# Wider steps in a planned first stage: conditioning rows by three row blocks, a channel-major projection by two

## The chip, the cores and the metric

One core of one Trainium2 chip runs the kernel. The metric is device time in microseconds (us) for one execution. The engines are named as in the profile: PE is TensorE's matmul side and PEld its weight loads, DVE is VectorE, ACT is ScalarE, POOL is GpSimd, SP is SyncE, which here only issues DMA transfers.

## The reference

One decoder layer on 512 tokens of width 1024, float32. Cut to what the change touches:

```
mod = silu(c) @ w_ada + b_ada                 # 1 x 6144: shift1, scale1, gate1, shift2, scale2, gate2
h = rmsnorm(x) * (1 + scale1) + shift1
proj = h @ w_in                               # 1024 x 2824: DeltaNet q, k, v (1536), its gate z (512), attention q, k, v, ...
q, k, v = silu(causal_conv(proj[:, :1536]))   # then a chunked gated delta rule over 8 chunks of 64 tokens
o_sw = sliding_window_attention(...)          # the other head group
x = x + gate1 * (concat(o_dn * silu(z), o_sw) @ w_out)
h = rmsnorm(x) * (1 + scale2) + shift2
x = x + gate2 * moe(h)                        # top 4 of 32 experts, 12.6 MB of weights each
```

## The kernel before

**Two stages.** The first stage (everything up to line 1608) computes the mixer and the routing; the second (from line 1900) runs the 32 experts, whose weights it streams from HBM. Between them the first stage's memory pools are closed, and the second stage's gathers need the routing result.

**The planner.** From line 445 on the order of the first stage's work is not written out by hand. Each piece of work is a Python generator (a task). It yields either a list of keys that it must wait for, or a claim: an engine letter (P for PE, V for DVE, S for ACT, G for POOL, D for a DMA), a cost in us, and tags of buffers that it takes. Class `Flow` (lines 113 to 180) plays the tasks against a model of the engines when the program is built and emits instructions in the order in which the model starts them. Among the claims that could start within `SLACK` (0.1 us) of the earliest one, the lowest priority number wins (line 173). After a claim the task's next claim is ready only a latency later (0.12 us for PE, 2.5 us for a DMA, line 117), so that two tasks that are both ready on PE take turns, claim by claim. A claim is never broken up: what the generator emits between two yields stands together in the engine's queue. On the chip every engine then runs its own queue in that order and waits by semaphores for real data.

**The late conditioning rows.** `late_loads` (line 630) loads w_ada for rows 2 to 5 of the six (gate1, shift2, scale2, gate2), eight blocks of 128 x 1024 (512 KB) for each row, into six slots (tag `lp`); SP issues them (line 637). `late(r)` (line 640) multiplies them: for each block k four matmuls on column strips of 32 (the program has eight matmul instructions for them, as each float32 matmul is two), line 649, then four more (again eight instructions) for the bias at line 654, an evacuation on DVE and a small store. Each block is a claim of its own on PE (0.5 us in the model) and so is the bias (0.45 us). The four rows follow one another; row r + 1 starts after the store of row r. Priority 1. The attention's `swa_weights` (line 732) wait for `("late", 5)`, since their buffer is one of the late rows' slots.

**The channel-major projection.** `project(c0, j)` (line 559) makes 128 channels by 512 tokens: for each of eight row blocks k three matmuls (`mm3`, line 314, emitted at line 317: high x high, high x low, low x high parts in fp32r) of 128 x 128 by 128 x 512 into `ps_ch`. Each k is a claim of 0.66 us on PE. There are 16 such projections: twelve for q, k and v (`conv`, priority 5) and four for the gate z (`gate`, priority 2), so 128 claims and 384 matmuls. `win` (line 538) loads their weights in 1 MB pieces on SP (line 542) and splits them on ACT, DVE and POOL.

**Around them** in the same planned list: `inverse` (line 976; the 64 x 64 triangular inverses of the delta rule, five levels of three 32-instruction matmul groups at line 818, then line 1033 and line 1049), the attention (`swa_*`, priority 1), the recurrence over eight chunks (`recur`), the output projection (lines 1142 and 1161) and the routing (`route`, `ranks`, `places`).

Of the kernel before, what the change touches and what calls it, by code (L numbers as in the profile page):

```python
# [20 lines left out]
P = 128  # L21
# [3 lines left out]
KT = D // P  # L25
# [9 lines left out]
THEN, THEN1 = 2, 6  # L35
RINGS = {"w": RING2 - 1, "x": 1, "r": RING, "v": RING3 - 1, "vy": 1, "e": RINGE}
SLACK = 0.1
CONV_END = "V"
PR = {"swa": 1, "conv": 5, "cend": 4, "in": 4, "late": 1, "z": 2, "load": 1, "yS": 7, "fin": 3, "rt": 4, "yT": 3, "rec": 1, "oout": 2}
UBANKS = 6  # L40
# [72 lines left out]
class Flow:  # L113
# [40 lines left out]
    def run(self):  # L154
        while True:
# [15 lines left out]
            else:  # L171
                first = min(at for at, _ in can)
                at, t = min((c for c in can if c[0] <= first + SLACK), key=lambda c: (c[1][0], c[0], c[1][1]))
                eng, cost = t[3][0][0], t[3][1]
# [9 lines left out]
def layer_kernel(ctx: ExitStack, tc: tile.TileContext, A, out, probe=None):  # L184
    nc = tc.nc
    V, S, G, TE = nc.vector, nc.scalar, nc.gpsimd, nc.tensor
# [5 lines left out]
    def bc(ap, shape):  # L192
        return ap.to_broadcast(shape)
# [23 lines left out]
    def bank(tag, name):  # L217
        return {"a": ppA, "d": ppD, "s": ppS, "o": ppO}[tag].tile([P, 512], F32, name=name, tag=tag)
# [7 lines left out]
    def wk(tag, name, bufs, n=T):  # L226
        return pool_of(tag).tile([P, n], F32, name=name, tag=tag, bufs=bufs)
# [68 lines left out]
    def behind(late, early):  # L296

        tc.add_manual_dep(late.ins, early.ins.name,
                          mybir.DependencyInfo(mybir.DependencyClass.NoSync, mybir.DependencyReason.DATA), reason="order")
# [14 lines left out]
    def mm3(acc, w, x_, start, stop):  # L314

        for q, (a, b) in enumerate(((0, 0), (0, 1), (1, 0))):
            TE.matmul(acc, lhsT=w[a], rhs=x_[b], start=start and q == 0, stop=stop and q == 2)  # L317

    cact = ce.tile([P, 8], F32, name="cact")
# [34 lines left out]
    hx = []  # L354
# [62 lines left out]
    with tc.manual_schedule(engines={nc.vector.engine, nc.scalar.engine, nc.tensor.engine}):  # L417
        for k in range(KT + 1):
# [22 lines left out]
            if k:  # L441
                for i in range(NT):
                    tok_mm(i, k - 1)
                mm3(tg[0:8], [w[:, 0:8] for w in wtok[k - 1]], hx[k - 1], k == 1, k == KT)
    flow = Flow({"a": 2, "d": 3, "s": 2, "o": 1, "cv": 4, "sv": 2, "x": 4, "r": 3, "m": 7, "L0": 1, "L1": 1, "lp": 6, "room": 2, "kv": 2, "sm": 2,
                 "qS": 2, "on": 2})

    def tv(n):
        return 0.09 + 0.001 * n
# [73 lines left out]
    kTv, wins = {}, {}  # L523

    def sigmoid(a, e):

        yield "S", ts(T)
        S.activation(e, a, AF.Abs)
        yield "S", ts(T)
        S.activation(e, e, AF.Exp, scale=-1.0)  # L530
        yield "S", ts(T)
        S.activation(e, e, AF.Ln, bias=one1)
        yield "V", tv(T)
        V.scalar_tensor_tensor(e, a, 0.0, e, op0=OP.min, op1=OP.subtract)
        yield "S", ts(T)
        S.activation(e, e, AF.Exp)
# [22 lines left out]
    def project(c0, j):  # L559

        a = None
        for k in range(KT):
            yield [("win", c0, k // 4)]
            yield ("P", 0.66) + (("a",) if k == 0 else ())
            if a is None:
                a = bank("a", "ps_ch")
            mm3(a, [w[:, P * j:P * j + P] for w in wins[c0, k // 4][k]], hx[k], k == 0, k == KT - 1)
        return a

    def conv_end(a, ct, dst, key):  # L570
# [12 lines left out]
        yield from sigmoid(y, e)  # L583
        yield CONV_END, (tg_ if CONV_END == "G" else tv)(T)
        (G if CONV_END == "G" else V).tensor_tensor(dst, y.rearrange("p (n c) -> p n c", c=64), e.rearrange("p (n c) -> p n c", c=64), op=OP.mult)
        flow.give("cv", "cv")
        flow.mark(*key)

    def conv(p, name, c0, prio):

        ct = c0 // P
        dst = None
        for j in range(2):
            a = yield from project(c0, j)
            if j == 0:
                if name == "q":
                    dst = qT[:, p]
                else:
                    yield "N", 0.0, "kv"
                    dst = kTv[name, p] = wk("kv", name + "T", 2, D).rearrange("p (n e c) -> p n e c", n=8, e=2)  # L600
            flow.add(prio, conv_end(a, ct + j, dst[:, :, j, :], ("head", name, p, j)))
        flow.give("x", "x", "r")
# [10 lines left out]
    def gate(p, prio):  # L613

        yield [("values", 2, 1)]
        if p == 0:
            state["zT"] = big("z", "zT", 2).rearrange("p (h t) -> p h t", t=T)
        for j in range(2):
            a = yield from project(1536 + 256 * p, j)
            flow.add(prio, gate_end(a, 2 * p + j))  # L620
        flow.give("x", "x", "r")
        flow.mark("zmm", p)
# [5 lines left out]
    lw = {}  # L628
# [11 lines left out]
    def late(r):  # L640

        pa = None
        for k in range(KT):
            yield [("lw", r, k)]
            yield ("P", 0.5) + (("o",) if k == 0 else ())
            if pa is None:
                pa = bank("o", "ps_ada")
            for j in range(4):
                TE.matmul(pa[32 * j:32 * j + 32, :256], lhsT=bc(cact[:, k:k + 1], [P, 32]), rhs=lw[r, k][:, 256 * j:256 * j + 256],
                          start=(k == 0), stop=False)  # L650
            flow.give("lp")
        yield "P", 0.45
        for j in range(4):
            TE.matmul(pa[32 * j:32 * j + 32, :256], lhsT=bc(ident[0:24, 4 * r + j:4 * r + j + 1], [24, 32]), rhs=bada, start=False, stop=True)
        yield ("V", tv(256)) + (() if r == 5 else ("sv",))
        m = g2s if r == 5 else wk("sv", "mod", 2)[:, 0:256]
        if r == 4:
            V.scalar_tensor_tensor(m, pa[:, :256], 1.0, n2q, op0=OP.add, op1=OP.mult)
        else:
            V.tensor_copy(m, pa[:, :256])  # L660
        flow.give("o")
        yield "D", 0.5
        nc.sync.dma_start(modd[r - 2].rearrange("(j n) -> j n", n=256), m.rearrange("(j r) n -> j r n", r=32)[:, 0])
        if r != 5:
            flow.give("sv")
        flow.mark("late", r)
# [889 lines left out]
    lp = once.enter_context(tc.tile_pool(name="lp", reuse_waits="tile", bufs=1))  # L1556
# [3 lines left out]
    with tc.manual_schedule(engines={nc.vector.engine, nc.scalar.engine, nc.tensor.engine, nc.gpsimd.engine, nc.sync.engine}):  # L1560
# [31 lines left out]
        flow.add(PR["swa"], swa())  # L1592
        flow.add(1, late_loads())
        flow.add(PR["late"], chain(*(late(r) for r in range(2, 6))))
        flow.add(PR["z"], chain(*(gate(p, PR["z"]) for p in range(2))))
        flow.add(PR["load"], loads())
# [304 lines left out]
    with tc.manual_schedule(engines={nc.sync.engine, nc.tensor.engine, nc.vector.engine, nc.scalar.engine}):  # L1901
# [10 lines left out]
        for q in range(NE + 1):  # L1912
            if q < NE:
                r = ORDER[q]
# [29 lines left out]
            if q:  # L1944
                r = ORDER[q - 1]
# [55 lines left out]
```

## Time and profile before

| | us |
|---|---|
| runs shown | 1479.09, 1485.01, 1486.35; median 1485.01 |
| profiled execution, its own time | 1480.72 |
| its span in the trace | 1478.9 |
| PE busy | 1381.5 (93% of the span) |
| PEld busy | 601.3 (41%) |
| DVE busy | 563.8 (38%) |
| mean HBM traffic over the span | 325 GB/s |

The profiled execution's own time is 1.8 us more than its span. An engine's busy time counts instructions under way; matmuls overlap, so that the time a matmul takes from PE is best read from the distance between the starts of neighbours. In a wait row, the name before the arrow is who waited and the name behind it is what ended the wait.

### The profile page before, as it was taken

How to read it: one execution, taken by the hardware profiler on the slowest of the kernel's cores; microseconds unless marked ns; L12 is line 12 of the kernel's file. 1: busy time of each engine (PE TensorE's matmuls, PEld its weight loads, DVE VectorE, ACT ScalarE, POOL GpSimd, SP SyncE). 2: the span in 40 equal slices, each digit the busy share in tenths (PEclk: the TensorE clock that was granted, in tenths of full speed). 3: DMA queues.
4: the chain of work that ended last, by engine and by line, in shares of the span. 5: the costliest groups of instructions: out<-in, count | busy, mean ns of one | idle time of the engine just before them, and what ended most of it. 6: DMA issues, size and time to landing. Idle time of an engine off the chain costs nothing. (4 is left out here: it accounts for less than half of the span.)

```text
span 1478.9 us, 22303 instructions
## 1 busy us (share of the span) xinstructions
PE 1381.5 (93%) x8586; PEld 601.3 (41%) x8586; DVE 563.8 (38%) x1247; ACT 237.8 (16%) x542; POOL 261.1 (18%) x216
## 2 busy tenths in 40 slices
PE   4999999999879999979999999999999999999974
PEld 3766666765443333322333333333333333343311
DVE  6965567566853222212221231223321323232310
ACT  4354354442211000000000000000000000010000
POOL 2213133202331111101011101102110112211110
PEclk9999999999969999999999999999999999999976
DMA  9655300256349999999999999999998999999995
GB/s 302 212 200 204 113 29 30 58 214 277 116 152 407 409 387 402 396 391 412 411 412 400 379 419 394 384 409 393 410 367 349 403 348 404 393 418 415 414 415 229
DMA packets 104980, 476.16 MB, mean 322 GB/s; under 512 B 13992, under 2 KB 39556, under 8 KB 55714
## 3 DMA queue, kind: packets, MB, share of 16 engines
q1 hardware_dynamic: 91842, 453.16, 77.4%
q0 software_dynamic: 11952, 18.75, 5.5%
q10 hardware_dynamic: 1072, 2.70, 0.5%
q8 instruction: 75, 1.23, 0.3%
q14 instruction: 39, 0.32, 0.1%
HBM read 464.14 MB, written 17.22 MB: 325 GB/s over the span
## 5 line engine op out<-in xcount | busy, mean ns | idle before, releaser
L1760 PE MATMUL ps_up<-we,xTe 128*64 128x512 f32 (+1 forms) x3040 | 622.2, 607 | 21.2 <-DMA we<-in_w_up_dram 16.8
L1760 PEld LDWEIGHTS ps_up<-we,xTe 128*64 128x64 f32 (+1 forms) x3040 | 188.5, 132 | 394.2 <-issue 336.8
L1797 PE MATMUL ps_dn<-we,aT 128*64 128x512 f32 (+1 forms) x1848 | 316.0, 534 | 19.7 <-DMA we<-in_w_down_dram 10.9
L1797 PEld LDWEIGHTS ps_dn<-we,aT 128*64 128x64 f32 (+1 forms) x1848 | 103.7, 129 | 232.2 <-issue 187.2
L1805 POOL DMA_INDIRECT out_dram<-yv,si x52 | 81.7, 1571 | 649.7 <-DVE yv L1804 464.9
L1712 DVE COPY xTe<-ps_xTe 128x256 f32<-128x256 f32 (+3 forms) x35 | 17.5, 501 | 307.4 <-PE ps_xTe L1711 307.4
L1785 ACT COPY aT<-ps_aT 128x512 f32<-128x512 f32 (+1 forms) x52 | 26.0, 530 | 512.5 <-PE ps_aT L1783 509.1
L1769 DVE TENSOR_TENSOR hu<-ps_up,bb 128x512 f32<-128x512 f32 (+1 forms) x52 | 32.1, 617 | 198.8 <-PE ps_up L1760 198.8
L1804 DVE SCALAR_TENSOR_TENSOR yv<-ps_dn,sg,g2p 128x512 f32<-128x512 f32 x38 | 28.5, 751 | 188.3 <-PE ps_dn L1797 187.4
L1771 ACT ACTIVATE hu<-hu 128x512 f32<-128x512 f32 (+1 forms) x52 | 29.8, 573 | 269.4 <-DVE hu L1770 269.4
L1697 POOL MEMSET xg<- 64x1024 f32 (+3 forms) x35 | 37.2, 1084 | 186.0 <-PE ps_xTe L1711 185.8
L317 PE MATMUL ps_ch<-hhi,wih 128*128 128x512 f32 x128 | 58.5, 457 | 0.0
L317 PE MATMUL ps_ch<-hl,wih 128*128 128x512 f32 x128 | 50.8, 397 | 0.0
L317 PE MATMUL ps_ch<-hhi,wl 128*128 128x512 f32 x128 | 50.5, 395 | 0.0
L1720 DVE STREAM_SHUFFLE bb<-bias 128x1024 f32<-128x1024 f32 (+1 forms) x44 | 48.8, 1137 | 0.1
L1712 ACT COPY xTe<-ps_xTe 128x256 f32<-128x256 f32 (+3 forms) x35 | 15.1, 433 | 163.4 <-PE ps_xTe L1711 163.4
L1698 POOL DMA_INDIRECT xg<-h2d,gi x35 | 35.7, 1021 | 16.1 <-POOL xg L1697 8.1
L1711 PEld LDWEIGHTS ps_xTe<-cst,xg 64*128 64x128 f32 (+3 forms) x280 | 24.1, 142 | 32.3 <-issue 23.1
L1783 PEld LDWEIGHTS ps_aT<-cst,act 128*128 128x128 f32 x180 | 24.3, 208 | 28.6 <-issue 25.7
L1711 PE MATMUL ps_xTe<-cst,xg 64*128 64x64 f32 (+3 forms) x280 | 30.1, 249 | 5.1 <-DMA xg<-h2d,gi 2.2
L317 PEld LDWEIGHTS ps_ch<-hhi,wih 128*128 128x128 f32 x128 | 24.2, 189 | 23.2 <-issue 18.0
L1142 PE MATMUL ps_y<-wos,oS 128*128 128x512 f32 x64 | 33.3, 613 | 0.0
(392 smaller groups left out, 1389.0 us busy)
## 6 DMA issues: line engine op xcount, KB each, us to landing
we<-in_w_up_dram SPq DMA_DIRECT2D x256, 1024.0 KB
we<-in_w_down_dram SPq DMA_DIRECT2D x128, 1024.0 KB
wa<-in_w_ada_dram SPq DMA_DIRECT2D x16, 512.0 KB
wi<-in_w_in_dram SPq DMA_DIRECT2D x8, 1024.0 KB
wl<-in_w_ada_dram SPq DMA_DIRECT2D x12, 512.0 KB
oS<-in_w_ada_dram SPq DMA_DIRECT2D x10, 512.0 KB
LL<-in_w_ada_dram SPq DMA_DIRECT2D x10, 512.0 KB
wt<-in_w_in_dram SPq DMA_DIRECT2D x4, 776.0 KB
```

The costliest lines, as they stand in the source:

```text
L317: TE.matmul(acc, lhsT=w[a], rhs=x_[b], start=start and q == 0, stop=stop and q == 2)
L1142: TE.matmul(a, lhsT=oS[:, j, P * i:P * i + P], rhs=wo[j][:, 512 * hf:512 * hf + 512], start=(j == 0), stop=(j == 3))
L1697: G.memset(xg[:rows_], 0.0)
L1698: state["gather"] = G.indirect_dma_start(out=xg[:rows_], out_offset=None, in_=h2d, in_offset=bass.IndirectOffsetOnAxis(ap=gidx(g)[:rows_], ...
L1711: TE.transpose(pt[:, k, :rows_], xg[:rows_, 512 * hf + P * k:512 * hf + P * k + P], ident[:rows_, :rows_])
L1712: state["turned", hf] = (S.copy if hf else V.tensor_copy)(xt_[:, 4 * hf:4 * hf + 4, :rows_], pt[:, :, :rows_])
L1720: V.stream_shuffle(bbs[w].rearrange("p h n -> p (h n)"), b[w], [0] * 32)
L1760: TE.matmul(t[w * j:w * j + w], lhsT=lhsT, rhs=rhs, start=(k == 0), stop=(k == KT - 1))
L1769: V.tensor_tensor(g, pg, bbs[w][:, 0], op=OP.add)
L1771: S.activation(sgm, g, AF.Sigmoid, scale=1.702)
L1797: TE.matmul(py[u][w * j:w * j + w, 0:m], lhsT=aT[u][:, kt % nf, w * (kt // nf):w * (kt // nf) + w], rhs=wd[kt][:, m * j:m * j + m], start= ...
L1805: G.indirect_dma_start(out=outv[u[1]], out_offset=bass.IndirectOffsetOnAxis(ap=sidx, axis=0), in_=yv, in_offset=None, compute_op=OP.add, b ...
```

## The change

`late` claims PE three times for a row, not nine: for blocks 0 to 2, blocks 3 to 5, and blocks 6 and 7 together with the bias. It waits for all blocks of a step before the step, and gives their slots back in the step. Its prices in the model are 0.25 + 0.17 for each block. `project` claims PE four times, not eight, for two row blocks each at 1.45. Nothing else is edited; the matmuls, their operands and their order within a row or a projection stay.

```diff
+LATES = {0: 3, 3: 6, 6: 8}
...
     def project(c0, j):
         a = None
-        for k in range(KT):
+        for k in range(0, KT, 2):
             yield [("win", c0, k // 4)]
-            yield ("P", 0.66) + (("a",) if k == 0 else ())
+            yield ("P", 1.45) + (("a",) if k == 0 else ())
             if a is None:
                 a = bank("a", "ps_ch")
-            mm3(a, [w[:, P * j:P * j + P] for w in wins[c0, k // 4][k]], hx[k], k == 0, k == KT - 1)
+            for k_ in (k, k + 1):
+                mm3(a, [w[:, P * j:P * j + P] for w in wins[c0, k // 4][k_]], hx[k_], k_ == 0, k_ == KT - 1)
         return a
...
         pa = None
         for k in range(KT):
-            yield [("lw", r, k)]
-            yield ("P", 0.5) + (("o",) if k == 0 else ())
+            if k not in LATES:
+                continue
+            ks = range(k, LATES[k])
+            yield [("lw", r, k_) for k_ in ks]
+            yield ("P", 0.25 + 0.17 * len(ks)) + (("o",) if k == 0 else ())
             if pa is None:
                 pa = bank("o", "ps_ada")
-            for j in range(4):
-                TE.matmul(pa[32 * j:32 * j + 32, :256], lhsT=bc(cact[:, k:k + 1], [P, 32]), rhs=lw[r, k][:, 256 * j:256 * j + 256],
-                          start=(k == 0), stop=False)
-            flow.give("lp")
-        yield "P", 0.45
+            for k_ in ks:
+                for j in range(4):
+                    TE.matmul(pa[32 * j:32 * j + 32, :256], lhsT=bc(cact[:, k_:k_ + 1], [P, 32]), rhs=lw[r, k_][:, 256 * j:256 * j + 256],
+                              start=(k_ == 0), stop=False)
+                flow.give("lp")
         for j in range(4):
             TE.matmul(pa[32 * j:32 * j + 32, :256], lhsT=bc(ident[0:24, 4 * r + j:4 * r + j + 1], [24, 32]), rhs=bada, start=False, stop=True)
```

## Rows read from the trace of the kernel before

**Rows 1.** The page, busy time of each engine, with share of the span and instructions.

```profile
PE 1381.5 (93%) x8586; PEld 601.3 (41%) x8586; DVE 563.8 (38%) x1247; ACT 237.8 (16%) x542; POOL 261.1 (18%) x216
```

**Rows 2.** Busy time by stretch, each engine, then PE clock, DMA share, GB/s.

```profile
79.10:170.20 91.10, 90.13 (x1044) 57.98 (x1043) 54.87 (x104) 36.93 (x67) 22.71 (x14) 1.00 0.59 209
170.20:240.00 69.80, 67.17 (x534) 46.66 (x531) 51.05 (x109) 37.49 (x95) 24.79 (x20) 0.98 0.10 31
240.00:312.00 72.00, 71.43 (x730) 50.13 (x728) 37.95 (x79) 32.35 (x72) 11.51 (x9) 1.00 0.26 73
312.00:410.00 98.00, 92.09 (x505) 48.29 (x506) 71.99 (x214) 22.20 (x84) 22.30 (x17) 1.00 0.55 208
436.00:1479.00 1043.00, 986.84 (x5379) 341.50 (x5379) 269.14 (x543) 72.20 (x140) 148.98 (x123) 0.97 0.99 391
```

**Rows 3.** Waits of PE from 79 to 440 us, the longest: total, times, longest.

```profile
PE ps_rt L1196 <- DVE room L1192: 7.5, 4, 2.7
```

**Rows 4.** Start of the second stage: POOL and SP in order of time.

```profile
430.23 0.18 POOL L1904 COPY second<-eri 1x1 int32<-1x1 int32 x1
...
431.47 11.94 SPq L1654 DMA_DIRECT2D we<-in_w_up_dram  x6
```

**Rows 5.** Tile of late rows: ns min/median/max of one, first and last start.

```profile
L649 PE MATMUL ps_ada<-wl,cact x96: 378/391/404, 86.4 to 168.4; 128*32 128x256 f32 x96
...
L649 PE MATMUL ps_ada<-oS,cact x80: 378/391/403, 90.2 to 161.9; 128*32 128x256 f32 x80
...
L649 PE MATMUL ps_ada<-LL,cact x80: 378/390/404, 93.9 to 164.5; 128*32 128x256 f32 x80
...
L654 PE MATMUL ps_ada<-bada,cst x32: 374/386/398, 103.6 to 169.9; 24*32 24x256 f32 x32
```

**Rows 6.** PE in order of time (start, us, line): late, projection, late.

```profile
140.05 0.64 PE L649 MATMUL ps_ada<-LL,cact 128*32 128x256 f32 x8
140.62 0.50 PE L317 MATMUL ps_ch<-hhi,wih 128*128 128x512 f32 x1
...
141.51 0.64 PE L649 MATMUL ps_ada<-wl,cact 128*32 128x256 f32 x8
```

**Rows 7.** PE in order of time: column strips by one column.

```profile
403.00 0.24 PE L1506 MATMUL ps_cnt<-one,sums 128*32 128x1 f32 x8
403.18 1.13 PE L1161 MATMUL ps_y<-wod,oT 128*128 128x512 f32 x2
```

**Rows 8.** The page, groups: experts' matmuls on half the columns; busy, mean ns.

```profile
L1760 PE MATMUL ps_up<-we,xTe 128*64 128x512 f32 (+1 forms) x3040 | 622.2, 607 | 21.2 <-DMA we<-in_w_up_dram 16.8
```

**Rows 9.** The page, groups: a third of the channel-major projection's matmuls.

```profile
L317 PE MATMUL ps_ch<-hhi,wih 128*128 128x512 f32 x128 | 58.5, 457 | 0.0
```

**Rows 10.** PE in order of time: inside an uninterrupted projection, one row block apart.

```profile
110.62 0.40 PE L317 MATMUL ps_ch<-hl,wih 128*128 128x512 f32 x1
...
111.32 0.40 PE L317 MATMUL ps_ch<-hl,wih 128*128 128x512 f32 x1
```

**Rows 11.** PE in order of time: a projection's row block ahead of transposes.

```profile
284.18 0.50 PE L317 MATMUL ps_ch<-hhi,wih 128*128 128x512 f32 x1
...
284.98 0.60 PE L934 MATMUL ps_tm<-cst,kT 128*128 128x128 f32 x4
```

**Rows 12.** SP in order of time: two loads of a late row.

```profile
139.10 1.97 SPq L637 DMA_DIRECT2D LL<-in_w_ada_dram  x2
```

**Rows 13.** The stretch after the first one's issue, columns as in rows 2.

```profile
139.10:142.00 2.90, 2.90 (x51) 1.68 (x50) 1.89 (x3) 0.06 (x1) 0.77 (x1) 1.00 0.58 172
```

**Rows 14.** SP's waits, 50 to 320 us: total, times, longest.

```profile
SPq L542 <- DVE wl L307: 46.4, 4, 26.3
```

**Rows 15.** PE in order of time: first attention weights; inverse's last products.

```profile
175.00 0.72 PE L743 MATMUL ps_l<-kS,qS 64*128 64x128 f32 x8
...
291.96 1.09 PE L1033 MATMUL ps_u<-vv,XT 64*64 64x128 f32 x16
...
294.57 1.09 PE L1033 MATMUL ps_u<-vv,XT 64*64 64x128 f32 x16
```

## The prediction, made before the changed kernel was run

> **What bounds the kernel now.** I read the page first: PE is busy in 93% of the span, no other engine above 38% [rows 1]. An average over two unlike stages decides nothing, so the busy time by stretch comes next [rows 2]. The second stage, from about 436 us, keeps the DMA at 0.99 of its time and PE at 987 of 1043 us; the change does not touch it. In the first stage, where the change lies, PE is busy 90.1 of 91.1 us, 67.2 of 69.8, 71.4 of 72.0 and 92.1 of 98.0, while the DMA stands at 0.10 to 0.59. The waits say the same: the longest group in which PE waited between 79 and 440 us is 7.5 us, all of it in routing, long after the edited tasks [rows 3]. So up to 410 us the first stage takes as long as PE's queue takes, and PE time that goes should bring its end forward.
>
> Does the end of the first stage carry the end of the kernel? The second expert's weights are requested by SP at 431.47, right after POOL's copy at 430.23 of an index that routing makes [rows 4]. The stream that fills the second stage thus starts when the first ends, and what the first stage gains or loses should arrive whole at the end.
>
> **The change part by part.** No matmul is added or removed. What goes is PE's turning from one kind of work to another.
>
> *Late rows.* The instructions are 96 + 80 + 80 for the blocks and 32 for the bias, 288 in all [rows 5]. In order of time each group on PE has eight and none sixteen, so there are 36 visits, from 86.4 to 169.9 us. A visit takes 0.57 us from its start to the next task's (140.05 to 140.62) [rows 6]: 36 x 0.57 = 20.5 us. After the change there are 12 visits of three groups each (3 blocks, 3 blocks, 2 blocks and the bias). The trace shows no visit of three, so I split the 0.57 into entering and streaming. A visit of eight instructions of the same tile shape with one column each takes 0.18 us (403.00 to 403.18) [rows 7]: nearly all entering, hence streaming of about 0.39. The experts' matmuls give a second price: 622.2 us for 3040 is 0.205 us for 512 columns on half the array's columns [rows 8]; a late instruction has half the columns and a quarter of the array, so 0.051, and eight take 0.41. I take 0.42 a group and 0.15 for entering: 3 x 0.42 + 0.15 = 1.41, twelve times 16.9. **Gain 3.6 us.** The bounds: nothing, if three groups take 3 x 0.57 (a longer time is excluded, since 0.57 already holds all that a visit needs), and 20.5 - 12 x 0.76 = 11.4, if the code's new price of 0.76 were true. I stay near rows 7 and 8, which agree.
>
> *Projection.* 128 row blocks, three matmuls each [rows 9]. Uninterrupted, one block follows the last after 0.70 us (110.62 to 111.32) [rows 10]. Alone between two late visits a block takes 0.89 (140.62 to 141.51) [rows 6], so a run costs 0.19 beyond its blocks; with transposes behind it 0.80, or 0.10 beyond [rows 11]. I take 0.17, as most runs stand between column strips or 64-wide tiles. Following PE in order of time from 79 to 308 us I count 76 runs: 49 of one block, 16 of two, 11 longer. After the change no run is shorter than two. If singles join in pairs (25), doubles stay (16) and longer ones stay (11), 52 runs are left: 24 x 0.17 = **4.1 us gain**. The bounds are nothing, if other tasks cut in so often that all 64 claims stand alone and find more tiled neighbours, and 6.8, if 40 runs are left at 0.19.
>
> *Loads and queues.* Late loads keep their number and size. Their slots come back in threes, so SP may issue them later, and weight pieces stand behind them on SP. Of a row's eight blocks six fit the slots; the last two are requested when the first visit gives slots back, so only the third visit of a row, four in all, is tight. From the issue at 139.10 [rows 12] to 142.0 the DMA moved 172 GB/s x 2.9 us, some 500 KB, one block [rows 13]: about 2.9 us for the first and 2 to 3 for the next. Between first and third visit lie the second (1.41) and two projection claims (1.59 each, two blocks and 0.19), at least 4.6 us. I take no stall, with 2.9 x 4 = 11.6 as the upper bound; a gain is excluded, for the loads do not wait for PE in the rows above. The projection's pieces wait for slots that their own split frees, 46.4 us in all [rows 14], so a few us on SP stay hidden; without that cover they would add to the 11.6.
>
> *Prices.* The model had 84.5 us for the projections (128 x 0.66) and 17.8 for the late rows, 102.3 together, where the trace needs 128 x 0.70 + 76 x 0.17 + 20.5 = 123. Now it has 92.8 + 8.4 = 101.2 against 115. PE's lag behind its model shrinks from 21 to 14 us; the other engines had that lag as slack. By itself I cost this at nothing, as PE remains behind; it is a reason for the first rival.
>
> **Sum.** 3.6 + 4.1 = 7.7 us, between 0 and 18. The profiled execution took 1480.7 us, 4.3 under the median of the runs; 1480.7 - 7.7 = 1473.0, and on the median of 1485.0 it is 1477.3. I forecast **1477 us**, its own range 1473 to 1481. A measurement of this kernel tells about 0.5% from no change, 7.4 us here, so the forecast lies on that line.
>
> **The rivals.**
>
> *More than the switches (1470).* Attention weights start on PE at 175.00 [rows 15], after the last late row. A row now needs three turns, not nine; with the turns of others between, some 2 us less for each row, 8 us in all. If attention also feeds the serial end of the stage, the list could close better by about as much again: 7.7 + 7. Against it: PE was full anyway, so earlier attention only displaces other work.
>
> *Half comes back as waits (1481).* DVE is busy 51 of 70 us and 72 of 98 in the later stretches [rows 2]. With less lag PE would wait for it more often, and half of the 7.7 is left.
>
> *PE was not the bound (1485).* By its weight loads PE is busy only 58.0 of the first 91.1 us [rows 2]; if that were the measure, a third of the stage would be room, and less switching would move no end. Against it, blocks in a run start at fixed distances [rows 10] and no wait of note is listed [rows 3]. The Trainium skill, Perfetto Trace Analysis, Identifying the Most-Contended Engine, says that matmul busy time is not a good measure of nearness to roofline and weight-load time is a better one; by that rule this rival would be the forecast. This trace agrees only so far as the switches are busy time without streaming.
>
> *Serial steps wait behind wider claims (1493, the other side).* Its place is the inverse of the second head pair and what follows, 236 to 304 us: five levels of three products and eight more steps, 23, each of which can find PE inside a projection. A claim that is one block longer delays it by up to 0.70, 16.1 in all; 16.1 - 7.7 = 8.4 us slower. It decides once filler work has run out before the chain ends: PE's idle time from 240 to 410, now 0.6 + 5.9 us [rows 2], would have to rise by over 15. Against it: the two products at 291.96 and 294.57 are 2.61 apart [rows 15], of which 1.59 is already a run of two blocks.
>
> *Late loads land late (1489).* The 11.6 above less 7.7.
>
> **How the numbers follow.** Forecast 0.44, more 0.18, half 0.14, not the bound 0.08, serial steps 0.13, loads 0.03. Faster by over 0.5%: a good half of the forecast's share (0.24), all of "more", a little of "half": 0.45. Slower: the serial steps and a part of the loads, 0.14. The rest, 0.41, is within. The range, 1466 to 1489, takes in "more" with 4 us below it and all cases but the serial one, and leaves out some 0.13 above and 0.05 below. The likeliest cases, all on the faster side or at none, span 1466 to 1485.
>
> **What would show it.** Right: 12 late visits of about 1.41 us; at most 64 projection runs, about 52; PE's busy share unchanged before 410; the second expert's weights requested near 424, not 431. Wrong: PE waiting for DMA at late rows; PE idle from 240 to 410 well above 6.5 us; or a request at 424 without an earlier end, which would mean that the second stage does not pass the gain on.

## The result, and the profile after

The changed kernel takes 1490.98 us (median of 7 runs, 1485.36 to 1494.51), the kernel before 1482.68 on the same chips (7 runs): a ratio of 1.0054, interval 1.0036 to 1.0072. It is slower by 0.54%, just past what a measurement can tell, where 1477 had been forecast. It is also above the range of 1466 to 1489. (The forecast was counted from 1485.0; counted from 1482.68 it would have been 1475.) The profiled execution took 1489.95 us, its span is 1488.2. The page's line of busy time (compare [rows 1]):

```profile
PE 1382.9 (93%) x8586; PEld 609.2 (41%) x8586; DVE 566.6 (38%) x1247; ACT 237.8 (16%) x542; POOL 256.7 (17%) x216
```

PE's busy time is the same within 1.4 us, so the page alone shows neither a gain nor a loss. The handoff between the stages, POOL's copy and SP's request in order of time:

```profile
440.53 0.18 POOL L1909 COPY second<-eri 1x1 int32<-1x1 int32 x1
...
442.17 0.57 SPq L1659 DMA_DIRECT2D we<-in_w_up_dram  x2
```

Against [rows 4] the copy is 10.3 us later, the request 10.7, the span 9.3. The whole loss is in the first stage. Its stretches, with the columns of [rows 2]:

```profile
79.10:170.20 91.10, 89.12 (x959) 63.88 (x957) 61.13 (x106) 41.05 (x73) 23.09 (x14) 0.96 0.55 201
170.20:240.00 69.80, 66.79 (x679) 48.00 (x678) 46.45 (x99) 35.29 (x81) 24.21 (x20) 0.98 0.13 42
240.00:312.00 72.00, 67.51 (x595) 47.19 (x594) 32.52 (x69) 28.12 (x69) 9.20 (x9) 0.93 0.28 86
312.00:410.00 98.00, 94.09 (x521) 51.07 (x519) 69.31 (x201) 23.48 (x88) 20.21 (x17) 0.95 0.47 179
```

The column that matters here is the one behind POOL's count, PE's granted clock. Before it read 1.00, 0.98, 1.00, 1.00; now 0.96, 0.98, 0.93, 0.95. The trace's clock record has two levels, 1.2 and 2.4 GHz, and stretches at the lower one. Here are the whole time from 79 us to the handoff and, under it, PE's stretches at half clock, of after and then of before:

```profile
79.00:440.53 361.53, 338.96 (x2915) 224.09 (x2914) 233.34 (x554) 132.74 (x328) 83.78 (x68) 0.93 0.37 133
126.30:133.10 6.80, 6.80 (x90) 4.26 (x89) 5.29 (x6) 2.90 (x5) 2.16 (x2) 0.51 0.88 329
225.30:228.70 3.40, 3.40 (x17) 1.48 (x14) 0.84 (x2) 2.46 (x4) 1.09 (x2) 0.51 0.00 0
245.80:256.00 10.20, 8.64 (x141) 7.84 (x138) 4.96 (x15) 5.25 (x18) 5.12 (x5) 0.50 0.01 2
331.10:341.30 10.20, 10.20 (x54) 7.50 (x52) 4.59 (x12) 1.18 (x6) 2.74 (x2) 0.50 0.00 0
419.80:423.20 3.40, 3.40 (x21) 1.84 (x22) 2.98 (x13) 1.15 (x4) 0.00 (x0) 0.52 0.00 0
426.70:440.53 13.83, 9.19 (x79) 6.13 (x79) 10.16 (x33) 1.22 (x7) 5.41 (x7) 0.50 0.11 39
```

```profile
79.00:430.23 351.23, 335.09 (x2915) 212.80 (x2915) 230.77 (x556) 132.65 (x329) 87.89 (x67) 0.97 0.39 136
213.50:216.90 3.40, 3.40 (x6) 1.34 (x6) 2.95 (x11) 1.24 (x4) 0.00 (x0) 0.50 0.00 0
414.80:430.23 15.43, 11.09 (x96) 8.14 (x88) 11.74 (x44) 1.35 (x9) 5.75 (x7) 0.50 0.18 69
```

**A ledger of the handoff** follows from these rows. The number of matmul instructions, 2915, is the same. PE is busy for 29.0 + 12.6 = 41.6 us at half clock after, for 14.5 before. I take half of that as lost (two attention products shown below take 1.90 us at half clock and 1.00 at full): 20.8 against 7.25, **+13.6**. PE's idle time is 361.53 - 338.96 = 22.6 against 16.1, **+6.4**. What is left, busy time less the lost half, is the work: 318.1 against 327.8, **-9.7**. The three sum to 10.3, as they must, since the ledger only divides the time up; whether the clock is a cause is a matter for the experiments. By it the work fell by somewhat more than forecast, and a slower clock and more idle time took it back twice over.

What came before those stretches? The longest waits of PE from 79 to 440 us, with two more of the routing left out at the dots (total, times, longest):

```profile
PE ps_rt L1201 <- DVE room L1197: 6.3, 5, 2.5
PE ps_X L823 <- DVE XT L988: 2.3, 1, 2.3
...
PE ps_Y L823 <- DVE X L1022: 1.9, 1, 1.9
...
PE ps_ss L848 <- ACT sq L843: 1.6, 1, 1.6
```

The first is that of [rows 3]. Each of the others stands just ahead of one of the first three stretches, and each is longer than any that PE had in the kernel before ahead of 360 us (1.15, at 211.1). PE in order of time for one of them:

```profile
224.50 1.29 PE L823 MATMUL ps_X<-cst,XT 64*64 64x64 f32 x32 [2.25 <-DVE XT L988]
225.72 1.97 PE L799 MATMUL ps_o<-pT,sw 128*64 128x512 f32 x2
227.62 0.80 PE L318 MATMUL ps_ch<-hhi,wih 128*128 128x512 f32 x1
```

PE finds nothing to do for 2.25 us, the clock falls at 225.3, and two attention products take 1.90 us to the next task's start (225.72 to 227.62). The 1.57 us at 123.94 (ps_ss) and the 1.85 at 245.30 (ps_Y) precede the other two. The fourth stretch, in the recurrence, has no wait ahead of it.

Where did the filler go? The q, k, v projections have priority 5 and wait for nothing but their weights and a buffer, so they are what the planner can put in when chains of short products wait. In the changed kernel they are done early: ACT begins to take up the last of them at 234.9, where it did so at 274.9 before. The gate's first block follows only at 270.58. For 36.7 us there is no projection block to fill with; before, the longest such time was 8.3 us (246.88 to 255.16, PE never idle in it).

```profile
233.91:270.58 36.67, 32.53 (x416) 22.61 (x415) 18.89 (x40) 13.54 (x33) 8.53 (x7) 0.86 0.13 30
```

In that hole lie 4.1 us of PE's idle time and the third stretch at half clock.

And the edit itself, in the same view:

```profile
144.64 1.07 PE L655 MATMUL ps_ada<-LL,cact 128*32 128x256 f32 x16
145.53 0.61 PE L655 MATMUL ps_ada<-wl,cact 128*32 128x256 f32 x8
146.08 0.49 PE L318 MATMUL ps_ch<-hhi,wih 128*128 128x512 f32 x1
...
147.66 0.64 PE L655 MATMUL ps_ada<-wl,cact 128*32 128x256 f32 x8
148.12 1.05 PE L655 MATMUL ps_ada<-oS,cact 128*32 128x256 f32 x16
149.10 1.09 PE L823 MATMUL ps_XT<-XT,Y 64*64 64x64 f32 x30
```

A late visit is 1.44 us (144.64 to 146.08, 147.66 to 149.10), a run of two row blocks 1.58. There are 12 such visits and 52 runs of projection blocks.

### The profile page after: what moved, and what is told of

It is laid out like the page before. It is cut to its first block, busy times and chain, and to the rows that moved or that the text cites. A ratio compares the mean times of both kernels' runs of the same rounds, so it can differ in the third digit from the quotient of the medians.

```text
span 1488.2 us, 22296 instructions
## 1 busy us (share of the span) xinstructions
PE 1382.9 (93%) x8586; PEld 609.2 (41%) x8586; DVE 566.6 (38%) x1247; ACT 237.8 (16%) x542; POOL 256.7 (17%) x216
## 5 line engine op out<-in xcount | busy, mean ns | idle before, releaser
L1788 PE MATMUL ps_aT<-cst,act 128*128 128x128 f32 x180 | 31.5, 306 | 2.3 <-DVE act L1780 1.9
```

What stands on the lines that cost most here:

```text
L1788: TE.transpose(pt[:, P * a:P * a + P], lv[:, a // 2, a % 2], ident)
```

## The experiments

There are two theories. **Clock and gaps**: the edit saves PE work as forecast, but the planned list is dealt anew, PE meets gaps in which no filler is ready, and the lost clock and idle time outweigh the gain. **Turns**: projections claim twice as much at each turn, so attention and the inverse come later, and the serial end of the stage with them, whatever the clock does. The table has the ledger of each kernel's profiled execution, worked out as above, in us against the kernel before: the handoff's move is the sum of the three columns behind it (PE's work at full clock, half of its work at half clock, its idle time). The last column has the medians, against the kernel before on the same chips:

| kernel | handoff | work | half clock | idle | median (ratio, interval) |
|---|---|---|---|---|---|
| after | +10.3 | -9.7 | +13.6 | +6.4 | +8.3 (1.0054, 1.0036 to 1.0072) |
| e1 late only | -3.9 | -7.1 | -0.2 | +3.4 | -2.8 (0.9983, 0.9967 to 0.9999) |
| e2 projection only | +6.5 | -6.6 | +7.8 | +5.2 | +6.7 (1.0048, 1.0026 to 1.0070) |
| e3 after, filled | +4.2 | -1.2 | +4.0 | +1.4 | -1.9 (0.9988, 0.9970 to 1.0006) |
| e4 held back 1 us | +2.7 | -8.0 | +2.4 | +8.3 | +2.9 (1.0028, 1.0010 to 1.0045) |
| e5 e3, recurrence filled | 0.0 | -0.3 | -1.1 | +1.3 | -2.9 (0.9990, 0.9978 to 1.0002) |
| e6 late and gate | -4.7 | -7.3 | +1.2 | +1.4 | -8.0 (0.9949, 0.9934 to 0.9965) |
| e7 e1, filled | -0.3 | -1.2 | +1.1 | -0.2 | -4.5 (0.9975, 0.9965 to 0.9985) |
| e8 prices only | +16.0 | -4.0 | +11.0 | +8.9 | +13.6 (1.0088, 1.0069 to 1.0107) |
| e9 change, old prices | +6.0 | -10.3 | +9.8 | +6.4 | +4.9 (1.0030, 1.0014 to 1.0045) |
| e10 change, measured prices | +8.7 | -10.7 | +15.4 | +4.0 | +6.2 (1.0042, 1.0028 to 1.0056) |
| e11 before, measured prices | +15.6 | 0.0 | +5.2 | +10.4 | +14.4 (1.0103, 1.0074 to 1.0132) |
| e12 e10, filled | +6.8 | -5.4 | +10.4 | +1.7 | +4.5 (1.0030, 1.0015 to 1.0045) |
| e13 e6, tail filled | +1.3 | +0.9 | +1.3 | -0.9 | -8.8 (0.9949, 0.9931 to 0.9966) |
| e14 e6 again | -4.6 | -7.1 | +0.9 | +1.6 | -8.7 (0.9949, 0.9932 to 0.9966) |

Filled kernels hold their added matmuls in the column of work. The halves are a rule of thumb, so the columns are good to some 2 us; handoff and idle are read directly. The ledger is of one execution for each kernel, which can lie some us from its median (e3's and e13's are their slowest).

### One part at a time

e1 keeps the projection's single claims at 0.66 and takes the late rows' wider steps; e2 is the other way round.

> Only the late rows in three claims; the projection keeps its single claims of 0.66. Theory of turns (longer claims and cheaper prices give the lowest-priority projections more of PE's turns, and the attention that feeds the serial end of the stage comes late): in the planned order 61 projection blocks stand ahead of the last late visit, against 54 before and 66 in the full change, so about half of the full change's loss less 3.6 us of saved turning: between 0 and +5 us against before. Theory of the late rows (their later end carries the loss): nearly the whole loss, +7 to +9. Theory of the clock (only PE time at half clock counts): minus 3.6 plus half of what stands at half clock between 100 and 400 us beyond the 3.4 us of before.

> Only the projection in claims of two blocks at 1.45; late rows as before. Theory of turns: the attention stands behind as many projection blocks as in the full change (78 to 116 ahead of its value products, against 63 to 105 before), so most of the loss without the late rows' gain: +6 to +12 us against before. Theory of the late rows: the projection's saved turning of 4 us is kept, minus 4. Theory of the clock: minus 4 plus half of the time at half clock beyond that of before.

e1: 1479.44 us, e2: 1488.97 (before 1482.25). So the late rows gain about what was forecast for them, 3.6, in the handoff (-3.9). In part that is luck: by the ledger the work fell by 7.1, and 3.4 came back as idle time. No loss came, neither the 0 to 5 that turns allowed nor the 7 to 9 of the late rows. Up to 400 us e1's clock never falls:

```profile
79.00:312.00 233.00, 227.96 (x2328) 159.74 (x2326) 150.94 (x298) 107.24 (x237) 59.36 (x44) 1.00 0.38 129
312.00:400.00 88.00, 81.72 (x442) 42.40 (x438) 67.19 (x188) 21.30 (x76) 19.33 (x16) 1.00 0.49 184
```

The loss comes with the projection, but in e2 not for the most part through the clock ahead of 400 us: e2's lower clock before 400 us (10.2 us of PE work at half) is worth only 3.4 more than before's. The rest is in its tail, PE in order of time:

```profile
397.21 1.10 PE L1162 MATMUL ps_y<-wod,oT 128*128 128x512 f32 x2
...
402.83 1.06 PE L1307 MATMUL ps_rt<-cst,rt 128*128 128x32 f32 x4 [2.58 <-DVE rt L1304]
...
408.60 3.77 PE L1197 MATMUL ps_rt<-room,rt 128*64 128x256 f32 x16
...
418.68 1.11 PE L1284 MATMUL ps_h2T<-cst,h 128*128 128x128 f32 x4 [2.53 <-DVE h L1280]
```

The last output projection starts at 397.21, where before's starts at 409.6, and yet the handoff, at 436.68, is 39.5 us behind it; before it was 20.6, in after 26.5. More of the routing is left for that end, and PE runs it at half clock (19.9 us of its work, before 11.0), with waits up to 2.9 us. So e2 speaks for the turns theory in part: its 6.7 lie in the range that turns gave (6 to 12), and a plan can lose its time in the tail too.

### Is it the clock? Matmuls added in the gaps

e3 is the changed kernel with 13 matmuls on constants, ahead of the products at which PE waited, in columns that nobody reads or that the next product overwrites. PE's order is otherwise that of the changed kernel.

```diff
+    def warm(dst, n):
+        for _ in range(n):
+            TE.matmul(dst, lhsT=ident, rhs=C("IOTA"), start=True, stop=True)
...
+                if p == 0 and z == 1 and j == 0:
+                    warm(ps[:, 256:512], 3)
...
+        if p == 1:
+            warm(pX[:, 0:256], 4)
...
+            if p == 1 and i in (2, 3):
+                warm(pY[:, 0:256], 4 if i == 2 else 2)
```

> The changed kernel with 13 extra matmuls of constants (about 0.43 us each) into unread columns where PE idles: three ahead of the third group of line 848, four ahead of the second pair's first inverse product, four and two ahead of its levels 2 and 3; the order is otherwise the same. Theory of the clock: the half-clock stretches at 126, 225 and 246 us (20.5 us in all) go or shrink, which gives back up to 10 us: minus 5 to minus 10 against the changed kernel, although work is added. Theory of turns alone: the attention and all that waits for it keep their place in the order, the extra work lies in idle time: between minus 2 and plus 1.

1480.38 us: with work added, 10.6 us less than the changed kernel (the theory of the clock gave 5 to 10, that of turns at most 2), and even with the kernel before. The same place as above, in e3:

```profile
220.44 1.89 PE L833 MATMUL ps_X<-cst 128*128 128x256 f32 x8
222.86 1.15 PE L823 MATMUL ps_X<-cst,XT 64*64 64x64 f32 x32 [0.53 <-DVE XT L994]
223.94 1.07 PE L799 MATMUL ps_o<-pT,sw 128*64 128x512 f32 x2
224.94 0.50 PE L318 MATMUL ps_ch<-hhi,wih 128*128 128x512 f32 x1
```

Four of the added matmuls, the fillers (x8, as each is two instructions), take 1.89 us of the 2.25 that stood empty, and the two attention products now take 1.00 us (223.94 to 224.94), not 1.90. From 79 to 312 us the clock is whole:

```profile
79.00:312.00 233.00, 228.76 (x2300) 162.44 (x2297) 142.26 (x280) 106.55 (x230) 56.47 (x43) 1.00 0.37 128
312.00:360.00 48.00, 47.90 (x309) 27.90 (x308) 33.95 (x109) 13.53 (x58) 7.41 (x5) 0.89 0.26 90
```

These rows and the ledger are of e3's slowest execution (1488.78). But the granted clock over the whole span is on record for every execution: 0.967 to 0.971 in the seven of the changed kernel, median 0.968; 0.971 to 0.980 in 31 of the kernel before, run beside e1 to e4, median 0.975; and in e3's ten the median is 0.9745. By a rough estimate from these numbers, (0.975 - 0.968) x 1480 = 10.4 us is what the lower clock costs the changed kernel, not in its profiled execution alone.

e7 is the control: the same 13 matmuls in e1, which has nothing to win back before 400 us.

> A control: e1 with the 13 constant matmuls of e3 in the same places of the program. e1 has no half-clock stretch in its first 400 us. Theory of the clock: nothing to give back there, 0 to plus 3 against e1 (5.6 us of added work, part of it in idle time). If filling helps in another way than by the clock: minus 2 or more.

1479.18 against e1's 1479.44; against the kernel before on their own chips -4.5 and -2.8, within each other's intervals. So there is no gain that can be told from none, where the same matmuls gave 10.6 us to the changed kernel: they help where the clock had fallen. **The loss of clock at those gaps is thus shown to be the larger part of what the change lost** (10.6 us net of the fillers' own cost, of the ledger's 13.6 + 6.4).

e5 adds four more (`warm(pb[:, 256:512], 2)` ahead of each of the router bias's two products), where e3's clock still falls, in the recurrence.

> The kernel of e3 with four more constant matmuls (0.43 us each, 1.7 us), two ahead of each small group of the router's bias, where the last half-clock stretch of the first 400 us stands (about 325 to 335 us, 10.2 us, in the profiles of the change and of e3) though PE is not idle there. Theory of the clock: the stretch goes, 5.1 gained less up to 1.7 of added work: 1475 to 1479 us, minus 2 to minus 5 against e3. Theory that only idle time brings the clock down, or that the recurrence is bound elsewhere: 0 to plus 2 against e3.

In its trace that stretch is whole (the row 312 to 360 of e3 above stands at 0.89):

```profile
312.00:360.00 48.00, 47.36 (x326) 27.30 (x329) 35.19 (x111) 14.79 (x60) 7.91 (x6) 1.00 0.35 126
```

Yet 1480.84 us is no better than e3, where 2 to 5 less were expected (against the kernel before on their own chips: -2.9 and -1.9). A trace shows one execution, and e3's was the slowest of its ten; whether the stretch stood in the other nine is not on record.

### Is it the planned order?

e4 lets the model hold a q, k, v projection back for 1 us between its claims, so that others get their turns (`W` is a claim on no engine, with a latency of 1.0 in the model).

```diff
+            if c0 < 1536 and k + 2 < KT:
+                yield "W", 0.0
```

> The changed kernel, but between two claims of a q, k or v projection the model holds the task back 1.0 us, so that other tasks get turns; matmuls and claims as in the changed kernel. In the planned order 50 blocks stand ahead of the last late visit (54 before, 66 in the change) and 58 to 102 ahead of the attention's value products (63 to 105 before). Theory of turns: the loss goes and the saved turning of 7.7 us remains, minus 9 to minus 17 against the changed kernel, 1474 to 1482 us. Theory of the late rows as such (few long visits are late whatever stands between): no change against the changed kernel. Theory of the clock: follows the time at half clock.

1485.18 us, 5.8 less than the changed kernel, and outside what either theory asked for: turns wanted 9 to 17, and the ledger's half clock falls by 11. The first attention weights start at 168.8, not 181.3 (before 175.00 [rows 15]), and little half clock is left ahead of 400 us (6.8 us of work, in the changed kernel 29.0), but PE's idle time is 8.3 over before's. An earlier attention by itself does not bring the gain.

e6 takes the late steps and doubles only the gate's projections; q, k and v keep single claims at 0.66.

```diff
+        kw = 2 if c0 >= 1536 else 1
+        for k in range(0, KT, kw):
...
+            yield ("P", 1.45 if kw == 2 else 0.66) + (("a",) if k == 0 else ())
```

> Late rows in three claims and the gate's four projections in claims of two blocks; the q, k and v projections keep single claims. The planned order is e1's up to the gate. Theory of the clock: no half-clock stretch before 400 us as in e1, and the gate's runs of one block, a few of them, save 0.19 us each: 0 to minus 2 against e1, 1477 to 1479.5 us. Theory of turns: wider gate claims stand in front of the chain from attention to recurrence (118 blocks ahead of the last value product, not 114): plus 1 to plus 4 against e1.

1475.68 us, and 1474.96 in e14: **it beats both kernels**, before by 8 us and after by 15. That is better than either theory gave (1477 to 1479.5, or more than e1), and why it gains that much more than e1 stays open. It differs from the changed kernel in nothing but the claims of the twelve q, k, v projections. Claiming their 96 row blocks in twos, length and price together, is what turned the gain round. In e6 the longest time without a projection block is 12.3 us, and PE is not idle in it.

Longer claims and new prices came together in the change. e8 is the kernel before with the new prices for its single claims (projection 0.725 a block; late 0.253 for blocks 0 to 5, else 0.197); e9 the change with the old prices; e10 with those its trace shows; e11 the kernel before with measured prices.

```
e8:  -  ("P", 0.66)                    +  ("P", 0.725)
e9:  -  ("P", 1.45)                    +  ("P", 1.32)
     -  ("P", 0.25 + 0.17 * len(ks))   +  ("P", 0.5 * len(ks) + (0.45 if k == 6 else 0.0))
e10: +  ("P", 1.59)  and  ("P", 1.43)
e11: +  ("P", 0.89)  and  ("P", 0.57)
```

> The kernel before with the change's prices alone, spread over its own claims: 0.725 for a projection block, 0.253 or 0.197 for a late block; every claim is as short as before. Theory that the length of the claims moves the attention back: as before, minus 2 to plus 2 against before. Theory of prices: the planned order already has 59 blocks ahead of the last late visit and 75 to 112 ahead of the attention's value products (63 to 105 before), so plus 4 to plus 9. Theory of the clock: plus half of the time at half clock beyond before's 3.4 us.

> The changed kernel with the claims' lengths as changed and the prices of the kernel before (late step 0.5 a block and 0.45 for the bias, projection 1.32 for two blocks). Its planned order is after's in kind: the last late visit stands behind 68 projection blocks (before 54, after 66), the attention's value products behind 80 to 116 (before 63 to 105, after 78 to 118). If the new prices are what turned the order round, it goes back to a gain against before: -1 to -8 us. If the longer claims by themselves do it (a projection takes twice as much of PE at each of its turns, while the others still take one short claim), it stays at after's: +4 to +12 us, with 15 us or more of half clock ahead of 400 us.

> The changed kernel with the prices that its own trace shows: late step 1.43, projection claim of two blocks 1.59. Planned order: last late visit behind 56 blocks (before 54, after 66), attention's value products behind 68 to 114. If order and filler decide (projections run ahead since they are too cheap in the model), the gain of the steps comes through: -3 to -8 us against before, under 8 us of half clock ahead of 400 us. If the longer claims alone cost, whatever the prices: +2 to +8 us.

> The kernel before, single claims, with the prices that its trace shows for a block or visit that stands alone: projection 0.89 a block, late 0.57 a block and for the bias. Planned order: last late visit behind 42 blocks (before 54), value products behind 56 to 92 (before 63 to 105), so more projection is kept back for the stretch from 230 us on. If filler kept back is worth time: -1 to -6 us against before, no more half clock ahead of 400 us than before's 3.4. If prices matter only by chance: within 3 us of before, either side. A plan in which the last projections bind the gate's part at the end of the delta rule would show as +3 to +10, with the recurrence's first products later than before's 304.9.

e8 is the worst but one at 1497.27 us, past the 4 to 9 us that were expected of prices: prices alone, not one claim longer, cost more than the whole change. Two of its four stretches at half clock ahead of the tail, the first with the time ahead of it:

```profile
175.20:182.00 6.80, 6.80 (x55) 5.06 (x48) 2.24 (x4) 1.33 (x3) 0.00 (x0) 1.00 0.00 1
182.00:192.20 10.20, 10.20 (x44) 6.97 (x44) 4.02 (x14) 2.29 (x8) 0.56 (x1) 0.50 0.01 2
311.80:318.60 6.80, 6.25 (x24) 3.19 (x26) 1.75 (x9) 1.47 (x7) 0.00 (x0) 0.50 0.94 383
```

e9 (1487.76) says that the longer claims lose without the new prices as well, e10 (1489.10) that prices as measured do not heal it, e11 (1497.32) that better prices make the kernel before slower by 14. My "filler kept back" falls with e11: ACT begins to take up its last q, k, v projection at 306.7 us (before 274.9), its attention is early (162.8), and it loses 10.4 us to idle time. The recurrence's first products start at 326.0 (before 304.9): the last of the three expectations had the place, but not the size. No rule on prices, claim lengths or early attention gave the sign. A hole of 34 to 37 us without a projection block, with PE idle for 2.9 to 4.1 us in it, stands in after, e2 and e9, but e8, e10 and e11 lose with none over 17.3 us. What the ledger shows in all six kernels without fillers that lose over 4 us (after, e2, e8, e9, e10, e11) is the same: half clock and idle time together cost 13 to 20 us more than before, and the work saved is 0 to 11.

### Does filling always help?

> The changed kernel with its measured prices (late step 1.43, projection claim 1.59) and 11 constant matmuls of 256 columns, about 0.43 us each and 4.7 us together, in the products' unread columns: 3 ahead of the first head pair's lengths of q (PE idle 0.78 us at 120.2 there, half clock from 122.0), 4 ahead of the second pair's (idle 2.66 at 216.2, half clock from 217.6), 4 in the router's bias inside the recurrence (half clock 323.4 to 333.6). Clock theory: these stretches shrink or go, worth up to 8.5 us less the part of the 4.7 that no idle time covers: 3 to 7 us less than the kernel without them (1489.1), so 1482 to 1486. If its loss is the order of the plan and not the clock, the time stays or rises: 1489 to 1493.

e12 (3 and 4 matmuls ahead of the q lengths of the two head pairs, 2 and 2 in the router's bias): 1488.12 us, about 1 less than e10, a miss for the clock theory. The three stretches aimed at went, but the one at 197 us in e10, which was left alone, is twice as long in e12, and a new one stands at 372.5: of the work at half clock before 400 us half went (20.5 to 10.2). The fillers' own work took that up, and e10's and e12's tail, of e2's kind (39.6 and 39.7 us from the last output projection to the handoff), stayed.

> The kernel with coarse late rows and the gate's projections by two, with 11 such matmuls in the routing of the last two token blocks, where PE waits for DVE: 4 ahead of the third block's table product (idle 1.61 us at 404.2), 2 ahead of the fourth's logits (0.98 at 410.2), 5 ahead of its table product (2.45 at 417.1). In every kernel so far PE runs at half clock from some 404 to 426 us on, with 11 to 25 us of work in it. Clock theory: the clock stays full past 404, the products of 2.2 us take about 1.1, and 1 to 4 us go: 1472 to 1475. If the tail's time is the chain over DVE and ACT, or the matmuls only stand in the way: within 1 us of the kernel without them, or up to 3 us more.

> The kernel with coarse late rows and the gate's projections by two once more, on the same chip as the one with the filled tail, to compare the two: 1474 to 1478, 4 to 9 us below the kernel before, as in its first runs. Outside of that, its first gain was the chip's and not the kernel's.

e13 (`warm(pte, i + 2)` ahead of the table products of blocks 2 and 3, two more ahead of block 3's logits) and e14 have the same median, 1474.91 and 1474.96. In the tail, from the last output projection to the handoff, first e13's row and then e14's:

```profile
405.78:431.54 25.76, 20.41 (x178) 14.28 (x177) 21.14 (x75) 3.85 (x16) 6.69 (x7) 0.93 0.23 83
```

```profile
399.05:425.65 26.60, 18.73 (x155) 12.48 (x155) 20.86 (x74) 3.52 (x16) 6.69 (x8) 0.67 0.21 82
```

The clock rose from 0.67 to 0.93 and gave back under 1 us (25.8 us, not 26.6). There DVE is busy more than PE in e14, and PE's waits in it are for DVE: half clock cost much where PE was the bound, and hardly anything here, where it waits. If that holds for other tails, the ledger's halves count too much there: the tail makes 0.8 of the 13.6 in the changed kernel, but some 4 of e2's 7.8 and 7 of e10's 15.4.

e13's profiled execution, its slowest (1482.08; the other five 1474.12 to 1476.09), shows what the clock does with no edit at all. Up to 400 us its PE instructions are e14's, in the same order; from 312 on, e13 and then e14:

```profile
312.00:400.00 88.00, 84.10 (x462) 45.35 (x463) 66.12 (x192) 21.26 (x81) 18.68 (x15) 0.96 0.46 174
```

```profile
312.00:400.00 88.00, 82.98 (x463) 43.76 (x462) 68.16 (x197) 22.73 (x83) 19.33 (x16) 1.00 0.49 183
```

Ahead of 400 us its clock fell at 127.5 and at 325.5, for 6.8 us each; e14's at 125.0, for 3.4 us. (13.6 - 3.4) / 2 = 5.1 us, and the handoffs are 5.9 apart, at 431.54 and 425.65.

## Why the prediction was wrong

*The first stage passes whole to the end*: right, with the other sign. The handoff moved by 10.3 us, the span by 9.3.

*Late rows*: right. 12 visits, at full clock 1.43 us each or, with the bias, 1.56 (e1 has all twelve at full clock), against 1.41 forecast; 8 x 1.43 + 4 x 1.56 = 17.7 where 16.9 was forecast, 0.8 us off the 3.6. (The upper bound of 11.4 took 0.76 for all twelve visits; the code has 0.59 for the four with the bias, which makes 12.1.)

*Projection*: right. 52 runs forecast, 52 found (40 of two blocks, 12 of four); between tiled neighbours a run of two takes 1.57 to 1.59, the figure used.

*Loads*: right. PE waited for no DMA at a late row.

*The work in sum*: 7.7 forecast, 9.7 in the ledger, within what the ledger is good for.

*Prices, and the sum*: here it failed. I wrote of the new prices and the shorter lag, "By itself I cost this at nothing, as PE remains behind", and of the whole stage, "PE time that goes should bring its end forward". With both I kept, without a term for them, two things that belong to an order of work and not to an operation: that PE finds filler at every step, and that it runs at the 0.98 to 1.00 of [rows 2]. The planner dealt the list anew, gaps of 1.57, 2.25 and 1.85 us appeared, and by the ledger half clock and idle time cost 13.6 + 6.4 us; e3 gave 10.6 us back by filling those gaps. That prices alone are not worth nothing e8 shows: on the single claims of the kernel before they cost 13.6 us. But they are not the whole of it either, as the change with the old prices (e9) still loses 4.9.

*The rivals.* "More" is refuted in its mechanism: the attention starts at 181.3, later than [rows 15], and the last bias product of the late rows at 176.5, where it stood at 169.9 [rows 5]. "Half comes back as waits" had something right: PE's idle time rose by 6.4 us, mostly in waits for DVE, but it had no term for the clock and so the wrong sign. "Serial steps", at 1493, had the sign, the place and nearly the size. Its condition came true, as filler ran out (from 233.9 to 270.6), but not its price: its mark was a rise of over 15 us in PE's idle time from 240 to 410, and the rows after give 4.5 + 3.9 = 8.4 against 6.5. The nearness of 1493 to 1491 is luck. "Late loads" falls with the loads. "Not the bound" falls too: in e6 PE's work is 7.3 us less, the handoff 4.7 earlier and the kernel 8.0 us faster. The Trainium skill, Perfetto Trace Analysis, Identifying the Most-Contended Engine, would have the headroom of TensorE judged by MFU and weight-load time; here the rows decide against that reading.

*My marks misled me.* "PE's busy share unchanged" was listed as a sign of being right. From 79 to 410 it hardly changed (317.6 us against 320.9), since work at half clock counts for nearly twice its time. Busy time has to be read with the clock beside it.

What stays open is which step of the planner makes an order with gaps, and how much of the idle time's 6.4 us would have been lost at full clock. Nine orders of this list were run besides the kernel before's, if the filled ones are left aside: e1's and e6's gained, the other seven lost.

## What to carry to other kernels

Where a program plans its own order from modelled costs, an edit of a cost or of a step's length is a new order, not a local saving: work out the saving, then allow for the whole list's gaps (nine orders here ran from -8 to +14 us on 1480), and try several orders. Sum an engine's busy time with its granted clock, since half clock hides in a full engine. Here wider steps gained for the late rows and the gate and lost for the q, k, v projections, which fill the others' gaps; that their use as filler is the reason fits the hole in the changed kernel, but no run shows it by itself.

## What the runs showed of the hardware

Added work made a kernel faster: 13 matmuls, some 6 us of PE at e3's 0.47 each (1.89 for four), took 10.6 us off. PE's clock fell to 1.2 GHz after idle times as short as 1.57 to 2.25 us. Idle time alone does not tell when: ahead of 400 us, in all the traces, the clock fell in, or within 2 us behind, each of the ten idle times of 2.03 to 2.80 us, but behind the twelve of 1.57 to 1.91 us only at some. In the kernel before it stayed full (1.00 in the last stretch of [rows 2]) behind this one:

```profile
369.32 1.44 PE L1196 MATMUL ps_rt<-room,rt 128*64 128x256 f32 x8 [1.86 <-DVE room L1192]
```

And of the 31 stretches at half clock ahead of 400 us eight began when PE had had no idle time over 0.15 us in the 8 us before (e8's at 182 us above is one). The recurrence of the changed kernel is another, PE in order of time:

```profile
328.57 1.95 PE L1213 MATMUL ps_sb<-cst,gm 128*128 128x1 f32 x16
...
333.15 3.62 PE L1220 MATMUL ps_sb<-fix,s2c 128*128 128x32 f32 x16
336.71 1.12 PE L1404 MATMUL ps_ws<-Sst,wT 128*64 128x128 f32 x8
```

PE is busy throughout (10.20 of 10.20 us from 331.1) at a clock of 0.50. The Trainium skill, TensorE: Matmul & The Clock Gate, Part 1: The HAM clock gate, says that half rate is the default and that activity releases it. The trace agrees at the three gaps and in e3; that a busy engine fell as well is what the fourth stretch adds. Half clock also comes and goes between executions of the same instructions (e13 and e14 up to 400 us), which there makes some 5 us of the 7 by which e13's slowest execution lies above its median.
